# The second k-tile's weights split and multiplied by halves at the start of a hybrid encoder block

## The chip, the cores and the metric

The kernel runs on one core of one Trainium2 chip. The time is the device time of one execution in microseconds (us); less is better. A profiled execution gives the span, from the first to the last instruction that the profiler saw, and the times of single instructions.

## The reference

One encoder block over 512 tokens of width 2048: a modulated RMS norm, one input projection for two token mixers (dilated attention and gated linear attention), gates, an output projection and a final norm. The change touches only the first lines:

```python
mod = jax.nn.silu(c) @ w_cond[layer] + b_cond[layer]
shift, scale, gate = jnp.split(mod, 3, axis=-1)
h = rms_norm(x) * (1.0 + scale[:, None]) + shift[:, None]
proj = h @ w_in[layer]
```

The attention's values, 1024 of the columns of `proj`, are the first product that the kernel computes.

## The kernel before

Tokens lie transposed: 16 k-tiles of 128 features (on partitions) by 512 tokens. A float32 product is made of three matmuls on upper and lower parts (`hi`, `lo`, in the type that TensorE reads at once): upper tokens by upper weights, lower tokens by upper weights, upper tokens by lower weights. In the opening, "stage a", `h_hi` and `h_lo` hold the tokens times (1 + scale), without the norm and the shift, which come in later. For k-tile k this needs

- `sums(k, 0)` (on VectorE, DVE): the scale of the k-tile's 128 features, one reduction over a 128 x 2048 block of `w_cond` (`cb`, a load of 1 MB) against silu(c) (`sb`). For k = 0 it is done in four quarters.
- `u_high(k)` (on ScalarE, ACT) and `u_low(k)` (on DVE): the upper part `h_hi` and the rest `h_lo`. Both put the even tokens into the first 256 columns and the odd ones into the last.
- `w_high("a", k)` (ACT) and `w_low("a", k)` (DVE): the upper and lower part of the weights, 128 x 1024 from a load of 0.5 MB (`rawa`). For k = 0 these are two halves of 512 columns.
- `square(k)` (ACT) and `add_square(k)` (DVE): the sum of squares for the norm, used only at the end of the stage.

TensorE (PE) then does 24 matmuls of 128 x 512, into eight PSUM tiles that stay open over the 16 k-tiles: four groups of 128 tokens by two halves of 512 columns. For k-tile 0 `first_products(z, e)` does them by half z and by kind e (0: upper by upper, 1: lower tokens, 2: lower weights), four at a time; for the others `products("a", k, j)` does the three kinds of one PSUM tile, one after the other, in lines 228, 229 and 230.

Each engine runs its instructions strictly in the order in which the program lists them, and that order is made in advance by a planner, `_plan`. Every step is a task with an engine, an assumed duration, the tasks that it depends on, a priority, and a buffer pool from which it takes or to which it gives. `_plan` goes through time: whenever an engine is free, it takes the task of the highest priority among those that are ready at that moment; it never leaves an engine idle for a more urgent task that would be ready soon. A result is ready for another engine 0.2 us after its task ends, that of a load 0.9 us after. Loads (SP's queue) are planned in the same way, one at a time. The engines begin at PE 9.0, ACT 8.0, DVE 5.3, loads 5.0. The plan's times only make the order; on the chip semaphores hold the engines.

```python
for n in after[x]:
    left[n] -= 1
    e = tasks[n][0]
    lat = 0.0 if tasks[x][0] == e else 0.9 if tasks[x][0] == "DMA" else 0.2
    at[n] = max(at[n], now + lat)
...
for n in sorted(waiting[e], key=lambda n: -tasks[n][3]):
    _, dur, _, _, _, take, give = tasks[n]
    if at[n] > now + 1e-6 or (take and not free[take]):
        continue
```

Tasks are named `sum`, `uh`, `ul`, `wh`, `wl`, `sq`, `ss` (`add_square`) and `load`, `x`, `w` for the loads of `cb`, tokens and weights. By the code's own costs the loads of the opening are planned as `load` 1 (5.0), `x` 1 (8.1), `w` 1 (8.88), `load` 2 (10.43 to 13.53), `w` 2 (13.53), `x` 2 (15.08), `w` 3 (15.86 to 17.41), `load` 3 (17.41). DVE's plan: `sum` 0, `wl0` 0, `ul` 0, `wl0` 1, `sum` 1 (11.15), `wl` 1 (13.57), `ul` 1 (14.74), `sum` 2 (15.44), `wl` 2 (17.86), `ul` 2 (19.03), `ss` 1, `wl` 3 (20.38), `sum` 3 (21.55), `ss` 2, `ss` 3, `wl` 4 (25.27), `ul` 3 (26.44), `sum` 4 (27.14). ACT's: `wh0` 0 (8.0), `uh` 0, `wh0` 1, `sq` 0, `sq` 1, `wh` 1 (11.34), `uh` 1 (13.77), `wh` 2 (15.98), `sq` 2, `uh` 2 (18.06), `wh` 3 (18.72). A weight load has four buffers (`raw`), the split weights three (`whi`, `wlo`).

Of the kernel before, what the change touches and what calls it, by code (L numbers as in the profile page):

```python
# [10 lines left out]
F32 = mybir.dt.float32  # L11
F32R = mybir.dt.float32r
I32 = mybir.dt.int32
AF = mybir.ActivationFunctionType
# [4 lines left out]
P = 128  # L19
# [170 lines left out]
def block_kernel(ctx: ExitStack, tc: tile.TileContext, a: dict):  # L190
    nc = tc.nc
# [14 lines left out]
    def T2(name, dt=F32, parts=P):  # L206
        return t2.tile([parts, 512], dt, tag="t2", name=name)
# [10 lines left out]
    mm = nc.tensor.matmul  # L218
    tt = nc.vector.tensor_tensor
    stt = nc.vector.scalar_tensor_tensor  # L220
    act = nc.scalar.activation
# [60 lines left out]
    hot = T2("hot", F32R)  # L282
    onesr = cst.tile([P, P], F32R, tag="ones", name="ones")
# [15 lines left out]
    with tc.manual_schedule(engines=PLANNED):  # L299
        small_inputs()  # L300
        cond_load(0, 0)
        half_load(0)
        x_load(0)
        half_load(1)
        nc.scalar.preload_act_table_set("silu_and_others")
        nc.vector.memset(hot.bitcast(F32), 1.0)
        nc.vector.memset(epst, EPS)
        nc.vector.memset(ch.bitcast(F32), 0.0)
        nc.vector.memset(sel.bitcast(F32), 0.0)
        nc.gpsimd.memset(cl.bitcast(F32), 0.0)  # L310
        warm(5)

        nc.vector.tensor_copy(ch[:4], cin[:, :512])
        act(sel[:4], cin[:, 512:], AF.Copy)
        tt(cl[:4], cin[:, :512], ch[:4].bitcast(F32), op=ALU.subtract)

        nc.vector.tensor_scalar(bcond[:, 16:32], bcond[:, 16:32], 1.0, None, op0=ALU.add)
        nc.vector.tensor_copy(onesr, hot[:, :P].bitcast(F32))
        for j in range(4):
            spread(j, ch, True)  # L320
            spread(j, cl, False)
            act(sb[:, 512 * j:512 * j + 512], pcs[j], AF.Silu)
        warm(6)
# [31 lines left out]
    h_hi = hp.tile([P, KT, 512], F32R, tag="h", name="h_hi")  # L355
    h_lo = hp.tile([P, KT, 512], F32R, tag="h", name="h_lo")
# [7 lines left out]
    raws, wts, low, last = {}, {}, set(), {}  # L364
# [135 lines left out]
    def task(name, eng, dur, deps, prio, fn, take=None, give=None):  # L500
        tasks[name] = (eng, dur, deps, prio, fn, take, give)

    x_of = lambda k: xt[k // 4][:, k % 4, :]
    spl, psb, vraw, vv, sqs = {}, {}, {}, {}, {}
    scale = cst.tile([P, KT], F32, tag="scale", name="scale")
# [18 lines left out]
    def halves_of(t):  # L524
        return t.rearrange("p (a c) -> p a c", a=2)

    def parities_of(t):
        return t.rearrange("p (c a) -> p a c", a=2)

    def u_high(k):  # L530
        act(halves_of(h_hi[:, k, :]), parities_of(x_of(k)), AF.Copy, scale=scale[:, k:k + 1])

    def u_low(k):
        stt(halves_of(h_lo[:, k, :]), parities_of(x_of(k)), scale[:, k:k + 1], halves_of(h_hi[:, k, :].bitcast(F32)),
            op0=ALU.mult, op1=ALU.subtract)
# [3 lines left out]
        act(sqs[k], x_of(k), AF.Square)  # L539

    def add_square(k):
        tt(ssum, ssum, sqs.pop(k), op=ALU.add)

    def sum_row():
# [23 lines left out]
    def w_high(st, k, c=slice(0, 1024)):  # L568
        if (st, k) not in spl:
            spl[st, k] = [wp.tile([P, 1024], F32R, tag="w" + e, name=f"s{st}{k}{e}") for e in ("hi", "lo")]  # L570
        act(spl[st, k][0][:, c], start_w[st, k][:, c], AF.Copy)

    def w_low(st, k, c=slice(0, 1024)):
        hi, lo = spl[st, k]
        tt(lo[:, c], start_w[st, k][:, c], hi[:, c].bitcast(F32), op=ALU.subtract)

    def first_products(z, e):

        (wh, wl), hh, hl = spl["a", 0], h_hi[:, 0, :], h_lo[:, 0, :]
        c = slice(512 * z, 512 * z + 512)  # L580
        for i in range(4):
            j, t = 4 * z + i, slice(P * i, P * i + P)
            if e == 0:
                psb["a", j] = PJ(f"sta{j}") if j < 5 else PA(f"sta{j}")
            mm(psb["a", j], (hl if e == 1 else hh)[:, t], (wl if e == 2 else wh)[:, c], start=e == 0, stop=False)

    def products(st, k, j):
        if k == 0:
# [43 lines left out]
    for i, (st, k) in enumerate(sets[1:], 1):  # L632
        e = "ab".index(st)
# [6 lines left out]
    for k in range(KT):  # L640
        task(("sum", k, 0), "DVE", 2.42 if k else 3.4, [("load", k, 0)] + ([("ul", 0)] if k == 1 else []), 600 - 2 * k,
             lambda k=k: sums(k, 0), None, "b8")
        task(("uh", k), "ACT", 0.66, [("sum", k, 0), ("x", k)], 900 - k, lambda k=k: u_high(k))
        task(("ul", k), "DVE", 0.7, [("uh", k)], 900 - k, lambda k=k: u_low(k))
        task(("sq", k), "ACT", 0.56, [("x", k)] if k else [("uh", 0)], 700 - k, lambda k=k: square(k))
        if k:
            task(("ss", k), "DVE", 0.65, [("sq", 0), ("sq", k), ("ss", k - 1)], 300 - k,
                 lambda k=k: add_square(k))
    for z in range(2):
        c = slice(512 * z, 512 * z + 512)  # L650
        task(("wh0", z), "ACT", 0.66, [("uh", 0)] if z else [], 910, lambda c=c: w_high("a", 0, c),
             None if z else "wts")
        task(("wl0", z), "DVE", 0.69, [("wh0", z), ("sum", 0, 0)] + ([("ul", 0)] if z else []), 899,
             lambda c=c: w_low("a", 0, c), None, "raw" if z else None)

    behind = {("a", 1): [("wh0", 1), ("wl0", 1)], ("a", 2): [("wh0", 1), ("wl0", 1)], ("b", 1): [("hi", 0), ("lo", 0)],
              ("b", 2): [("wh", "b", 1), ("wl", "b", 1)], ("b", 3): [("wh", "b", 2), ("wl", "b", 2)]}
    for i, (st, k) in enumerate(sets):
        if not i:
            continue  # L660
        gh, gl = [[x] for x in behind[st, k]] if (st, k) in behind else ([], [])
        task(("wh", st, k), "ACT", 1.0, [("w", st, k)] + gh, 640 - i, lambda st=st, k=k: w_high(st, k), "wts")
        task(("wl", st, k), "DVE", 1.17, [("wh", st, k)] + gl, 640 - i, lambda st=st, k=k: w_low(st, k),
             None, "raw")
# [13 lines left out]
    for z in range(4):  # L678
        task(("row", z), "ACT", 0.9, [("uh", 7 + z), "rowl"], 50, lambda z=z: row_part(z // 2, z % 2))
    one_before = []  # L680
    for z in range(2):
        for e in range(3):
            name = ("mm", "a", 0, 7) if (z, e) == (1, 2) else ("m0", z, e)
            task(name, "PE", 1.2, one_before + [("uh", 0), ("wh0", z)] + [[], [("ul", 0)], [("wl0", z)]][e], 100, lambda z=z, e=e: first_products(z, e), None,
                 "wts" if (z, e) == (1, 2) else None)
            one_before = [name]
    for i in range(n):
        if i > 7:
            mm_task(i)
        st, k, j = chain[i]  # L690
        if k == KT - 1:
            task(("vo", j), "ACT", 0.54, [("mm", "a", k, j)], 950, lambda j=j: v_out(j))
# [13 lines left out]
    for i in range(n, 2 * n):  # L706
        mm_task(i)
        st, k, j = chain[i]
# [3 lines left out]
    for w in range(4):  # L712
        for kt in range(4):
            j, g = w // 2 * 4 + kt, w % 2
# [739 lines left out]
    for e in "hl":  # L1454
        t = hp.tile([P, KT, 512], F32R, tag="h", name="c_" + e)
# [318 lines left out]
```

## Time and profile before

| | |
|---|---|
| median of 3 runs | 910.82 us (909.99 to 911.43) |
| the profiled execution | 910.26 us, span 908.5 us |
| granted TensorE clock, mean | 0.997 |
| busy: PE, DVE, ACT, POOL | 894.6, 727.5, 492.9, 113.8 us |

In the lines shown below, PE is a matmul, PEld the load of its stationary operand, DVE VectorE, ACT ScalarE, POOL GpSimd, SP the queue that issues most loads. A line has the source line, the engine, the operation, and output <- inputs by the program's names with their shape. In the table of stretches the columns are the stretch, its length, busy time with the number of instructions of PE, PEld, DVE, ACT and POOL, the granted TensorE clock as a share of the full one, the busy share of the DMA engines, and GB/s. A busy PE is not PE at its peak, since the ends of matmuls are modelled; starts are what to compare.

### The profile page before, as it was taken

To read this page: it belongs to the slowest core of one execution; us is meant where nothing else is said; L and a number is where in the kernel's file an instruction comes from. 1 tells how busy PE (TensorE), PEld (TensorE's weight loads), DVE (VectorE), ACT (ScalarE), POOL (GpSimd) and SP (SyncE) were. 2 spreads that over 40 slices of the span, in tenths; PEclk is the share of its full clock that TensorE was granted. 3 is DMA by queue.
4 is the path that set the end of the run, shared out by engine and by line. 5 is a ranking of instruction groups with operands and counts; after the bars stand their busy time and mean duration, and the time that the engine had idled before them with its cause. 6 is when DMAs were issued, how large, how long until landed. Compare 5 with 4: busy or idle time off the path is not lost.

```text
span 908.5 us, 12576 instructions
## 1 busy us (share of the span) xinstructions
PE 894.6 (98%) x4295; PEld 746.9 (82%) x4295; DVE 727.5 (80%) x1235; ACT 492.9 (54%) x855; POOL 113.8 (13%) x203
## 2 busy tenths in 40 slices
PE   8999999999999999999999999999999999999996
PEld 6888888888888888888878888888888888888884
DVE  7988799878879888888659668495787559797797
ACT  5553533565655655655658554373654238455464
POOL 0000000023312222222100101111120100000001
PEclk9999999999999999999999999999999999999998
DMA  9999498588688898997878979778796987887863
GB/s 348 402 413 400 181 356 316 167 247 229 202 267 250 239 254 243 240 283 209 275 242 257 319 199 312 210 232 273 230 282 200 278 288 277 294 286 254 298 233 143
DMA packets 64203, 241.30 MB, mean 266 GB/s; under 512 B 8357, under 2 KB 10693, under 8 KB 54537
## 3 DMA queue, kind: packets, MB, share of 16 engines
q1 hardware_dynamic: 57378, 198.18, 61.1%
q0 software_dynamic: 6464, 42.01, 20.0%
q8 instruction: 34, 0.56, 0.2%
q10 hardware_dynamic: 296, 0.30, 0.1%
q14 instruction: 31, 0.25, 0.1%
HBM read 224.64 MB, written 51.47 MB: 304 GB/s over the span
## 4 chain that ended last, share of the span: by engine, by line
PE 92%; DVE 3%; ACT 2%; DMA 1%; issue 1%; SPq 0%; DVEq 0%; ACTq 0%
PE ps_qk L228 5%; PE ps_qk L229 5%; PE ps_qk L230 5%; PE g L230 4%; PE g L229 4%; PE g L228 4%; PE o L886 3%; PE stb L230 3%; PE stb L228 3%; PE stb L229 3%; PE ps_ag L228 3%; PE ps_ag L230 3%; PE ps_ag L229 3%; PE ps_gv_P L228 3%; PE ps_gv_P L229 3%; PE ps_gv_P L230 3%
## 5 line engine op out<-in xcount | busy, mean ns | idle before, releaser
L327 DVE CUSTOM_DVE_ANT_0 cb<-cb,sb,c_bcond 128x2048 f32<-128x2048 f32 (+1 forms) x32 | 73.4, 2295 | 0.3 <-DMA cb<-in_wm 0.3
L842 POOL TENSOR_SCALAR p<-p,st 128x416 f32<-128x416 f32 (+2 forms) x93 | 47.3, 516 | 175.2 <-DVE st L834 133.1
L831 ACT ACTIVATE p<-p,st 128x416 f32<-128x416 f32 x64 | 41.0, 641 | 39.5 <-DVE st L827 37.1
L861 ACT ACTIVATE pt<-t 128x384 fp32r<-128x384 f32 x64 | 31.2, 487 | 31.0 <-PE t L857 30.5
L428 POOL DMA_DIRECT2D T<-in_w_o x32 | 23.1, 723 | 157.9 <-ACT V2h L492 10.8
L886 PEld LDWEIGHTS o<-pt,vv 128*128 128x128 f32 x256 | 34.4, 189 | 4.2 <-DVE pt L862 1.7
L862 DVE TENSOR_TENSOR pt<-t,pt 128x384 fp32r<-128x384 f32 x64 | 35.1, 549 | 2.5 <-ACT pt L861 2.0
L886 PE MATMUL o<-pt,vv 128*128 128x256 f32 x256 | 35.9, 283 | 0.1
L857 PEld LDWEIGHTS t<-c_ident,p 128*128 128x128 f32 x192 | 24.8, 140 | 8.6
L857 PE MATMUL t<-c_ident,p 128*128 128x128 f32 x192 | 31.3, 272 | 0.0
L827 DVE CUSTOM_DVE_ANT_0 p<-s,g 128x160 f32<-128x160 f32 x64 | 23.5, 367 | 7.2 <-PE s L820 6.3
L827 DVE CUSTOM_DVE_ANT_0 p<-s,g,st 128x256 f32<-128x256 f32 x64 | 27.6, 431 | 1.6
L327 DVE CUSTOM_DVE_ANT_0 rawg<-rawg,crow,gate 128x1024 f32<-128x1024 f32 x16 | 20.4, 1280 | 4.1 <-DMA rawg<-in_wg 4.1
L820 PE MATMUL s<-ks,ql 128*128 128x416 f32 x64 | 22.5, 352 | 0.0
L819 PE MATMUL s<-ks,qh 128*128 128x416 f32 x64 | 22.5, 352 | 0.0
L1057 ACT ACTIVATE sq<-st,sc 128x256 f32<-128x256 f32 x24 | 12.2, 506 | 18.4 <-DVE st L1047 9.9
L428 POOL DMA_DIRECT2D T3V<-in_w_gv x8 | 5.5, 687 | 126.0 <-ACT qk21h L492 119.8
L1547 POOL TENSOR_SCALAR x<-x,rn 128x512 f32<-128x512 f32 x2 | 2.3, 1164 | 148.0 <-ACT rn L1536 143.6
L327 DVE CUSTOM_DVE_ANT_0 rawg<-rawg,crow,c_bcond 128x1024 f32<-128x1024 f32 x16 | 20.3, 1279 | 0.1
L877 DVE TENSOR_TENSOR pt<-r,pt 32x128 fp32r<-32x128 f32 x64 | 17.8, 279 | 1.9 <-ACT pt L875 1.3
L428 POOL DMA_DIRECT2D T<-T x16 | 9.1, 571 | 79.9 <-ACT V8h L492 12.9
L562 ACT ACTIVATE h_hi<-xt,shift 128x512 fp32r<-128x512 f32 x16 | 11.5, 719 | 12.9 <-DVE shift L327 12.9
(1660 smaller groups left out, 3129.6 us busy)
## 6 DMA issues: line engine op xcount, KB each, us to landing
cb<-in_wm SPq DMA_DIRECT2D x31, 1024.0 KB, 9.0
T<-in_w_o POOLq DMA_DIRECT2D x32, 512.0 KB, 6.6
rawg<-in_wg SPq DMA_DIRECT2D x32, 512.0 KB, 5.8
raw_O<-in_w_o SPq DMA_DIRECT2D x32, 512.0 KB, 4.4
raw_qk<-in_w_qk SPq DMA_DIRECT2D x24, 512.0 KB, 4.6
raw_O<-T SPq DMA_DIRECT2D x24, 512.0 KB, 5.0
rawb<-in_w_sb SPq DMA_DIRECT2D x16, 512.0 KB, 5.4
rawv<-in_wv SPq DMA_DIRECT2D x16, 512.0 KB, 4.4
```

The lines of the kernel that those rows point to most:

```text
L228: mm(ps, lh, rh, start=first, stop=False, skip_group_check=more)
L229: mm(ps, ll, rh, start=False, stop=False, skip_group_check=more)
L230: mm(ps, lh, rl, start=False, stop=last, skip_group_check=more)
L327: return nc.vector.tensor_tensor_reduce(out=w, in0=w, in1=with_, op0=ALU.mult, op1=ALU.add, scale=1.0, scalar=init, accum_out=dst)
L428: move = nc.gpsimd.dma_start(dst, src, max_dma_last_dim=8192, **how).ins
L827: top = nc.vector.tensor_tensor_reduce(out=t[:, lo:hi], in0=ps[:, lo:hi], in1=gt[h][:, at:at + 2 * (hi - lo) - 1:2], op0=ALU.add, op1=ALU.min,
L831: act(t, t, AF.Exp, bias=st[:, 0:1], scale=-1.0, accum_out=st[:, 1:2])
L842: last["pool"] = nc.gpsimd.tensor_scalar(to, of, st[:, 2:3], 1.0, op0=ALU.mult, op1=ALU.mult).ins
L857: nc.tensor.transpose(pk[:, kt * P:kt * P + P], t[:, first_ + kt * P:first_ + kt * P + P], ident)
L861: act(hi, src, AF.Copy)
L862: tt(lo, src, hi.bitcast(F32), op=ALU.subtract)
L886: mm(po[:, :256], vv[h // 4][:, CHUNK_OF[e][c], h % 4, :], t[:, w, c, :], start=n_ == 0 and w == 0, stop=n_ == 3 and w == 1)
```

## The change

The weights of k-tile 1 are split in two halves of 512 columns, as those of k-tile 0 were: tasks `wh1` and `wl1` take the place of `wh` and `wl` of k-tile 1. Its 24 matmuls are done by `first_products(1, z, e)`, half by half, four at a time, with the kinds in the order upper by upper, lower weights, lower tokens. `u_high` of k-tiles 0 and 1 becomes two instructions of 256 columns. The upper token part of k-tile 1 now also depends on the upper half 0 of its weights, the lower one on the lower half 0; the splits of k-tile 2 depend on those of half 1 of k-tile 1. The copy that makes the matrix of ones leaves the start of DVE's list and stands ahead of the first `add_square`; each `add_square(k)` now waits for `u_low(k)` in the plan.

```diff
--- before.py
+++ after.py
@@ -315,7 +315,6 @@
         tt(cl[:4], cin[:, :512], ch[:4].bitcast(F32), op=ALU.subtract)
 
         nc.vector.tensor_scalar(bcond[:, 16:32], bcond[:, 16:32], 1.0, None, op0=ALU.add)
-        nc.vector.tensor_copy(onesr, hot[:, :P].bitcast(F32))
         for j in range(4):
             spread(j, ch, True)
             spread(j, cl, False)
@@ -528,7 +527,9 @@
         return t.rearrange("p (c a) -> p a c", a=2)
 
     def u_high(k):
-        act(halves_of(h_hi[:, k, :]), parities_of(x_of(k)), AF.Copy, scale=scale[:, k:k + 1])
+        to, of = halves_of(h_hi[:, k, :]), parities_of(x_of(k))
+        for c in ((slice(0, 1), slice(1, 2)) if k < 2 else (slice(0, 2),)):
+            act(to[:, c], of[:, c], AF.Copy, scale=scale[:, k:k + 1])
 
     def u_low(k):
         stt(halves_of(h_lo[:, k, :]), parities_of(x_of(k)), scale[:, k:k + 1], halves_of(h_hi[:, k, :].bitcast(F32)),
@@ -539,6 +540,8 @@
         act(sqs[k], x_of(k), AF.Square)
 
     def add_square(k):
+        if k == 1:
+            nc.vector.tensor_copy(onesr, hot[:, :P].bitcast(F32))
         tt(ssum, ssum, sqs.pop(k), op=ALU.add)
 
     def sum_row():
@@ -574,15 +577,15 @@
         hi, lo = spl[st, k]
         tt(lo[:, c], start_w[st, k][:, c], hi[:, c].bitcast(F32), op=ALU.subtract)
 
-    def first_products(z, e):
-
-        (wh, wl), hh, hl = spl["a", 0], h_hi[:, 0, :], h_lo[:, 0, :]
+    def first_products(k, z, e):
+
+        (wh, wl), hh, hl = spl["a", k], h_hi[:, k, :], h_lo[:, k, :]
         c = slice(512 * z, 512 * z + 512)
         for i in range(4):
             j, t = 4 * z + i, slice(P * i, P * i + P)
-            if e == 0:
+            if e == k == 0:
                 psb["a", j] = PJ(f"sta{j}") if j < 5 else PA(f"sta{j}")
-            mm(psb["a", j], (hl if e == 1 else hh)[:, t], (wl if e == 2 else wh)[:, c], start=e == 0, stop=False)
+            mm(psb["a", j], (hl if e == 1 else hh)[:, t], (wl if e == 2 else wh)[:, c], start=e == k == 0, stop=False)
 
     def products(st, k, j):
         if k == 0:
@@ -640,11 +643,11 @@
     for k in range(KT):
         task(("sum", k, 0), "DVE", 2.42 if k else 3.4, [("load", k, 0)] + ([("ul", 0)] if k == 1 else []), 600 - 2 * k,
              lambda k=k: sums(k, 0), None, "b8")
-        task(("uh", k), "ACT", 0.66, [("sum", k, 0), ("x", k)], 900 - k, lambda k=k: u_high(k))
-        task(("ul", k), "DVE", 0.7, [("uh", k)], 900 - k, lambda k=k: u_low(k))
+        task(("uh", k), "ACT", 0.66, [("sum", k, 0), ("x", k)] + ([("wh1", 0)] if k == 1 else []), 900 - k, lambda k=k: u_high(k))
+        task(("ul", k), "DVE", 0.7, [("uh", k)] + ([("wl1", 0)] if k == 1 else []), 900 - k, lambda k=k: u_low(k))
         task(("sq", k), "ACT", 0.56, [("x", k)] if k else [("uh", 0)], 700 - k, lambda k=k: square(k))
         if k:
-            task(("ss", k), "DVE", 0.65, [("sq", 0), ("sq", k), ("ss", k - 1)], 300 - k,
+            task(("ss", k), "DVE", 0.65, [("sq", 0), ("sq", k), ("ss", k - 1), ("ul", max(k, 1))], 300 - k,
                  lambda k=k: add_square(k))
     for z in range(2):
         c = slice(512 * z, 512 * z + 512)
@@ -652,11 +655,15 @@
              None if z else "wts")
         task(("wl0", z), "DVE", 0.69, [("wh0", z), ("sum", 0, 0)] + ([("ul", 0)] if z else []), 899,
              lambda c=c: w_low("a", 0, c), None, "raw" if z else None)
-
-    behind = {("a", 1): [("wh0", 1), ("wl0", 1)], ("a", 2): [("wh0", 1), ("wl0", 1)], ("b", 1): [("hi", 0), ("lo", 0)],
+        task(("wh1", z), "ACT", 0.66, [("w", "a", 1), ("uh", 1) if z else ("wh0", 1)], 901, lambda c=c: w_high("a", 1, c),
+             None if z else "wts")
+        task(("wl1", z), "DVE", 0.69, [("wh1", z), ("ul", 1) if z else ("wl0", 1)], 898.5,
+             lambda c=c: w_low("a", 1, c), None, "raw" if z else None)
+
+    behind = {("a", 2): [("wh1", 1), ("wl1", 1)], ("b", 1): [("hi", 0), ("lo", 0)],
               ("b", 2): [("wh", "b", 1), ("wl", "b", 1)], ("b", 3): [("wh", "b", 2), ("wl", "b", 2)]}
     for i, (st, k) in enumerate(sets):
-        if not i:
+        if (st, k) in (("a", 0), ("a", 1)):
             continue
         gh, gl = [[x] for x in behind[st, k]] if (st, k) in behind else ([], [])
         task(("wh", st, k), "ACT", 1.0, [("w", st, k)] + gh, 640 - i, lambda st=st, k=k: w_high(st, k), "wts")
@@ -678,14 +685,15 @@
     for z in range(4):
         task(("row", z), "ACT", 0.9, [("uh", 7 + z), "rowl"], 50, lambda z=z: row_part(z // 2, z % 2))
     one_before = []
-    for z in range(2):
-        for e in range(3):
-            name = ("mm", "a", 0, 7) if (z, e) == (1, 2) else ("m0", z, e)
-            task(name, "PE", 1.2, one_before + [("uh", 0), ("wh0", z)] + [[], [("ul", 0)], [("wl0", z)]][e], 100, lambda z=z, e=e: first_products(z, e), None,
-                 "wts" if (z, e) == (1, 2) else None)
-            one_before = [name]
+    for k in range(2):
+        for z in range(2):
+            for e in ((0, 1, 2), (0, 2, 1))[k]:
+                name = ("mm", "a", k, 7) if (z, e) == (1, 2 - k) else ("m", k, z, e)
+                task(name, "PE", 1.2 if k == 0 else 0.91, one_before + [("uh", k), (f"wh{k}", z)] + [[], [("ul", k)], [(f"wl{k}", z)]][e],
+                     100, lambda k=k, z=z, e=e: first_products(k, z, e), None, "wts" if (z, e) == (1, 2 - k) else None)
+                one_before = [name]
     for i in range(n):
-        if i > 7:
+        if i > 15:
             mm_task(i)
         st, k, j = chain[i]
         if k == KT - 1:
```

## The prediction

> **What bounds the kernel now.** I read the page first, then the waits of PE, then the opening in stretches, then each engine's timeline there. In the timelines the columns are start, duration, engine, line, instruction, and in brackets the idle time just before with its releaser.
>
> ```profile
> span 908.5 us, 12576 instructions
> ...
> PE 894.6 (98%) x4295; PEld 746.9 (82%) x4295; DVE 727.5 (80%) x1235; ACT 492.9 (54%) x855; POOL 113.8 (13%) x203
> ...
> PE 92%; DVE 3%; ACT 2%; DMA 1%; issue 1%; SPq 0%; DVEq 0%; ACTq 0%
> ```
> ```profile
> PE sta L585 <- ACT h_hi L531: 2.1, 1, 2.1
> PE warm L294 <- DVE hot L306: 1.5, 1, 1.5
> PE sta L229 <- DVE h_lo L534: 0.7, 1, 0.7
> PE go L1089 <- ACT V27h L492: 0.3, 1, 0.3
> ```
> ```profile
> 10.17:15.75 5.58, 5.58 (x24) 4.61 (x25) 4.56 (x5) 3.34 (x5) 0.00 (x0) 1.00 1.01 413
> 15.75:28.10 12.35, 11.56 (x50) 8.94 (x48) 12.24 (x15) 6.20 (x8) 0.00 (x0) 1.00 1.03 415
> 28.10:60.00 31.90, 31.90 (x141) 26.41 (x142) 30.23 (x33) 17.72 (x30) 0.69 (x1) 1.00 1.02 405
> ```
>
> TensorE carries 92% of the chain that ended last, and of its named waits only 0.3 us lies behind the opening. From 28.10 to 60 us it is busy for 31.90 of 31.90 us. So what the change is worth is the move of one moment: when PE enters its last unbroken run, at about 28 us. In 15.75 to 28.10 VectorE (the third engine of the row) is busy for 12.24 of 12.35 us and the DMA share is full: there DVE's order decides.
>
> ```profile
> 10.17 1.20 PE L585 MATMUL sta<-sa0hi,h_hi 128*128 128x512 f32 x4 [2.13 <-ACT h_hi L531]
> 11.20 1.08 PE L585 MATMUL sta<-sa0hi,h_lo 128*128 128x512 f32 x4
> ...
> 15.75 0.40 PE L228 MATMUL sta<-sa1hi,h_hi 128*128 128x512 f32 x1
> 16.82 0.50 PE L229 MATMUL sta<-sa1hi,h_lo 128*128 128x512 f32 x1 [0.67 <-DVE h_lo L534]
> ```
> ```profile
> 27.59 0.39 PE L228 MATMUL sta<-sa3hi,h_hi 128*128 128x512 f32 x1
> 28.10 0.49 PE L229 MATMUL sta<-sa3hi,h_lo 128*128 128x512 f32 x1
> 28.44 0.39 PE L230 MATMUL sta<-sa3lo,h_hi 128*128 128x512 f32 x1
> ```
>
> From 11.20 to 15.75 twenty matmuls start: 0.2275 us each, 5.46 us for the 24 of a k-tile. The second matmul of k-tile 1 should start at 15.98 and starts at 16.82, 0.84 late, for the low token part `h_lo`. In k-tile 3 the second starts 0.28 late, again for `h_lo`, and the next follows after 0.34 instead of 0.23. PE without that wait would have begun k-tile 3 at 28.44 - 2 x 0.2275 = 27.98; this is the moment I compare.
>
> **The order after the change.** Each engine's order comes from the planner in the code, from costs and due times written there, so I worked the changed tasks through by hand (plan times, which only give the order). Sum 1 ends on DVE at 13.57 as before. ACT splits half 0 of the second weights from 11.34 to 12.00; DVE takes their low half from 13.57 to 14.26. The upper token part runs on ACT from 13.77 to 14.43, so the low token part `ul` 1 is ready at 14.63. But the third modulation load ends at 13.53 and with its 0.9 makes sum 2 ready at 14.43. DVE is idle from 14.26, and the planner never holds an engine back for a more urgent task: it takes sum 2 (2.42) at 14.43, and `ul` 1, though of priority 899 against 596, comes behind it. Before, the undivided low part kept DVE until 14.74, when `ul` 1 was ready, and `ul` 1 went first. So DVE's new order is: low half 0, sum 2, `ul` 1, low half 1, `ul` 2, the moved copy and sum of squares, low part of k-tile 3, that of k-tile 2, sum 3, a sum of squares, low part 4, `ul` 3. Tile 3 comes ahead of 2 because the split of tile 2 now waits for low half 1 (ready at 18.44) and that of tile 3 for its load (18.31), ACT being idle.
>
> **Part by part, on the chip's rows.**
>
> ```profile
> 5.66 0.22 DVE L318 CAST ones<-hot 128x128 fp32r<-128x128 f32 x1
> 5.89 0.75 DVE L327 CUSTOM_DVE_ANT_0 cb<-cb,sb,c_bcond 128x512 f32<-128x512 f32 x1
> ...
> 9.24 0.69 DVE L575 TENSOR_TENSOR sa0lo<-rawa,sa0hi 128x512 fp32r<-128x512 f32 x1
> ```
> ```profile
> 9.36 0.76 ACT L531 ACTIVATE h_hi<-xt,scale 128x512 fp32r<-128x512 f32 x1 [1.22 <-DVE scale L327]
> ...
> 13.78 1.06 ACT L571 ACTIVATE sa1hi<-rawa 128x1024 fp32r<-128x1024 f32 x1 [0.64 <-DMA rawa<-in_w_sa]
> 14.75 0.75 ACT L531 ACTIVATE h_hi<-xt,scale 128x512 fp32r<-128x512 f32 x1
> ...
> 19.74 1.05 ACT L571 ACTIVATE sa3hi<-rawa 128x1024 fp32r<-128x1024 f32 x1
> ```
> ```profile
> L616 ACT ACTIVATE vv<-vraw,rcol 128x256 fp32r<-128x256 f32 x16 | 7.0, 495 | 0.0
> ```
>
> *Copy moved.* The first sum starts up to 0.22 earlier, and with it the chain to 9.36 (bounds 0 and 0.22; I take 0.18). *Token halves.* The nearest row for a half is the 128x256 at 0.495; two of them end some 0.14 to 0.24 later than one of 0.76, but the first matmuls read only half 0: PE starts at 9.18 + 0.50 + 0.05 = 9.73 instead of 10.17. The second half ends at 9.18 + 0.40 + 0.50 = 10.08 (ACT's steps overlap by 0.1, as 14.75 against 13.78 + 1.06 shows), `h_lo` some 0.8 later, and its product starts at 10.9 instead of 11.20. So k-tile 1 can begin at 10.9 + 4.55, about 15.5 instead of 15.75. *Weight halves.* The second weights still land at 13.76; half 0 is split by 14.40 and its low half by 15.1; the token halves end at 15.2. So the first eight matmuls of k-tile 1 (upper tokens with high and low weights) run from 15.5 to 17.3. The new order puts the `h_lo` product after them, 8 x 0.2275 = 1.8 us more room than before.
>
> ```profile
> SPq L273 <- DMA cb<-in_wm: 2.2, 1, 2.2
> ```
> ```profile
> 11.83 2.35 DVE L327 CUSTOM_DVE_ANT_0 cb<-cb,sb,c_bcond 128x2048 f32<-128x2048 f32 x1 [0.33 <-DMA cb<-in_wm]
> ...
> 14.88 1.22 DVE L575 TENSOR_TENSOR sa1lo<-rawa,sa1hi 128x1024 fp32r<-128x1024 f32 x1 [0.69 <-ACT sa1hi L571]
> 16.02 0.74 DVE L534 SCALAR_TENSOR_TENSOR h_lo<-xt,scale,h_hi 128x512 fp32r<-128x512 f32 x1
> 16.68 2.34 DVE L327 CUSTOM_DVE_ANT_0 cb<-cb,sb,c_bcond 128x2048 f32<-128x2048 f32 x1
> ...
> 18.95 1.22 DVE L575 TENSOR_TENSOR sa2lo<-rawa,sa2hi 128x1024 fp32r<-128x1024 f32 x1
> ...
> 20.76 0.68 DVE L542 TENSOR_TENSOR ssum<-ssum,sq 128x512 f32<-128x512 f32 x1
> 21.36 1.22 DVE L575 TENSOR_TENSOR sa3lo<-rawa,sa3hi 128x1024 fp32r<-128x1024 f32 x1
> ```
>
> *The wait that is added.* Sum 2 needs its 1 MB load. In the stretch 15.5 to 16.7 SP's queue has one wait, for such a load; its next issue starts at 16.29, so that load landed about 16.28 (bounds for sum 2's start: 16.3, and 16.68 where it stood). DVE, in order, stands idle from 15.1 with the finished `h_hi` of tile 1 behind it. Sum 2 holds DVE for 2.27 (16.68 to 18.95): to 18.58. `ul` 1 then ends at 19.33, and PE starts its product at 19.40: a new wait of 19.40 - 17.3 = 2.1 us. What was won earlier, the copy and the token halves, ends in this wait and is worth nothing.
>
> *Behind it.* PE: 13 matmuls are left of 16, counted from 19.40 with 0.34 for the first step: k-tile 2 at 19.40 + 0.34 + 15 x 0.2275 = 23.15 (before, 22.15). DVE from 18.58, by start-to-start steps of the rows: `ul` 0.66, low half about 0.65, `ul` 0.66, copy 0.22, squares 0.60, low part of tile 3 1.14, then that of tile 2, 1.22 long: it ends at 23.7, where PE wants it two matmuls into the tile, at 23.6. So 0.16 more and a restart of 0.11: k-tile 3 at 23.15 + 5.46 + 0.27 = 28.88. `h_lo` of tile 3 is due at 29.1; DVE ends it at 23.65 + 2.27 + 0.60 + 1.14 + 0.75 = 28.4: that old wait is gone. Sum: 28.88 - 27.98 = **+0.9 us**. Bounds: sum 2 at 16.68 adds 0.4; low part 2 on time takes 0.2 off, and 0.3 later adds that; together +0.4 to +1.6.
>
> ```profile
> 17.62 0.33 SPq L267 DMA_DIRECT2D rawa<-in_w_sa  x1
> ```
> ```profile
> 29.45 1.06 ACT L571 ACTIVATE sa5hi<-rawa 128x1024 fp32r<-128x1024 f32 x1 [1.69 <-DMA rawa<-in_w_sa]
> ```
>
> *What is hidden.* The load of tile 5's weights, issued at 17.62, reuses the buffer of tile 1's, which is now released at about 20.0. SP waits there, and a modulation load and a token load behind it. Weights issued at 17.62 land near 29.4, so some 11 us of transfers stand ahead, and a stall of 2.4 us lets none run dry: zero; were that cover gone, 2.4. In the later k-tiles the sums of squares trail by one tile on DVE; the same number of steps stand in a tile, so zero. The last one still ends before the row sum, which waits for an eviction.
>
> [...] PE was idle for 2.13 us ahead of 10.17, and its next four matmuls took 1.03 instead of 0.91 us: that restart, 0.12, is what I charge. [...]
>
> The profiled execution took 910.26 us (span 908.5 and 1.76 around it), so 911.2; the median of the three runs is 910.82, 0.56 higher, so the runs should have a median of **911.7**.
>
> **The rivals.**
> 1. *`ul` 1 runs ahead of sum 2*, as its priority suggests, and the change does what its words say. Then nothing waits in k-tiles 1 and 2. On DVE the copy (0.22) and the second half (2 x 0.69 against 1.22) are about paid for by half 0 being ready 0.44 before 14.88, so the steps behind keep their times but for one sum of squares fewer (0.7) ahead of this one:
>
> ```profile
> 27.30 0.75 DVE L534 SCALAR_TENSOR_TENSOR h_lo<-xt,scale,h_hi 128x512 fp32r<-128x512 f32 x1
> ```
> It then ends at 27.35 instead of 28.05, and PE loses 0.7 less at k-tile 3: 910.1. Against it: the 0.2 us by which the planner finds sum 2 ready first.
> 2. *The buffers of split weights go round in allocation order* (slower). Three buffers serve them; tile 3 is now split ahead of 2. If tile 5 gets the buffer of tile 3 and not of the one first free, ACT stands at its split until PE ends k-tile 3 at 34.3; the split ends at 35.4, its low part on DVE at 36.6 and `h_lo` of tile 4 behind that at 37.3, 2.8 after it is due (34.6). With a restart +3.8: 914.6. It decides only if that buffer comes free later than 29.4, when the weights land.
>
> ```profile
> 44.37 1.06 ACT L571 ACTIVATE sa8hi<-rawa 128x1024 fp32r<-128x1024 f32 x1 [1.57 <-PE sta L229]
> ```
> Such a wait exists, off the path here; that releases are taken in order of time speaks against the rival, as the planner counts them so.
> 3. *The clock falls in the new wait.* The opening shows both rates:
>
> ```profile
> 5.18 0.57 PE L297 MATMUL pc<-c_lo,sel 128*128 128x512 f32 x1
> 5.58 0.39 PE L297 MATMUL pc<-c_hi,sel 128*128 128x512 f32 x1
> 5.81 0.39 PE L297 MATMUL pc<-c_lo,sel 128*128 128x512 f32 x1
> ```
> 0.40 a matmul until 5.58, 0.23 from there, 4.1 us after PE began (its first wait ended at 1.5). A second such spell loses 4.1 x (1 - 0.23/0.40) = 1.7: +2.6, 913.4. The 2.13 us that left no such spell speak against it.
>
> **How the numbers follow.** A measurement of this kernel can tell about 0.2%, 1.8 us, from no change. Forecast 0.72, rival 1 0.11, rival 2 0.08, rival 3 0.04, something not named 0.05. The forecast lies inside 1.8 us but for 0.02 above it; rival 1 but for 0.01 below; rivals 2 and 3 are slower; the unnamed goes 0.02, 0.02, 0.01. Faster 0.03, same 0.82, slower 0.15. The range takes in the forecast's own bounds (911.2 to 912.4), rival 1 and the runs' spread, 0.8 us either way: 909.9 to 913.2; rivals 2 and 3 stay out.
>
> **What would show it.** Right: on DVE the 128x2048 sum of k-tile 2 starts near 16.3 ahead of `h_lo` of tile 1; PE waits about 2 us for that `h_lo` after the first eight matmuls of k-tile 1; no PE wait at k-tile 3, which begins near 28.8; PE starts near 9.7. Wrong: `h_lo` of tile 1 before 16.3, a k-tile 3 that begins before 28.0, a wait of ACT on PE near 29 to 34, or matmuls 0.4 apart behind the wait.

## The result and the profile after

The changed kernel took 912.51 us (median of 21 runs, 911.15 to 915.23), the kernel before 911.05 in the same series (21 runs, 909.99 to 912.20). The ratio is 1.0017, 95% interval 1.0010 to 1.0025: slower by about 1.5 us. The interval is clear of 1, but the difference is still below the 0.2% (1.8 us) under which the prediction spoke of no change. The forecast was 911.7, its range 909.9 to 913.2. The profiled execution took 912.51 us. From its page:

```profile
span 910.5 us, 12568 instructions
...
PE 896.2 (98%) x4295; PEld 745.9 (82%) x4295; DVE 727.8 (80%) x1236; ACT 493.9 (54%) x858; POOL 113.9 (13%) x203
...
PE 91%; DVE 3%; DMA 3%; ACT 1%; issue 1%; SPq 0%; DVEq 0%; ACTq 0%
```

All of PE's named waits after the change (us in total, times, longest):

```profile
PE sta L588 <- ACT h_hi L532: 1.7, 1, 1.7
PE sta L588 <- DVE h_lo L535: 1.5, 1, 1.5
PE warm L294 <- DVE hot L306: 1.5, 1, 1.5
PE go L1097 <- ACT V27h L491: 0.3, 1, 0.3
```

The 0.7 us for `h_lo` in k-tile 3 is gone; 1.5 for another `h_lo` stands in its place. DVE's timeline in the opening shows which, and why:

```profile
14.39 0.69 DVE L578 TENSOR_TENSOR sa1lo<-rawa,sa1hi 128x512 fp32r<-128x512 f32 x1 [0.25 <-ACT sa1hi L574]
16.22 2.35 DVE L326 CUSTOM_DVE_ANT_0 cb<-cb,sb,c_bcond 128x2048 f32<-128x2048 f32 x1 [1.14 <-DMA cb<-in_wm]
18.50 0.08 DVE L326 DVE_READ_ACCUMULATOR2_ANT scale<- 128x1 f32 x1
18.50 0.74 DVE L535 SCALAR_TENSOR_TENSOR h_lo<-xt,scale,h_hi 128x512 fp32r<-128x512 f32 x1
...
20.50 0.75 DVE L535 SCALAR_TENSOR_TENSOR h_lo<-xt,scale,h_hi 128x512 fp32r<-128x512 f32 x1
21.17 1.22 DVE L578 TENSOR_TENSOR sa2lo<-rawa,sa2hi 128x1024 fp32r<-128x1024 f32 x1
22.30 1.22 DVE L578 TENSOR_TENSOR sa3lo<-rawa,sa3hi 128x1024 fp32r<-128x1024 f32 x1
```

DVE stands idle for 1.14 us for the load of sum 2, although ACT has finished `h_hi` of tile 1 at about 15.2; the sum then holds it for 2.28, and `h_lo` of tile 1 starts at 18.50. On PE (timeline):

```profile
16.69 1.07 PE L588 MATMUL sta<-sa1lo,h_hi 128*128 128x512 f32 x4
19.30 1.20 PE L588 MATMUL sta<-sa1hi,h_lo 128*128 128x512 f32 x4 [1.54 <-DVE h_lo L535]
...
23.07 0.39 PE L228 MATMUL sta<-sa2hi,h_hi 128*128 128x512 f32 x1
...
28.50 0.39 PE L228 MATMUL sta<-sa3hi,h_hi 128*128 128x512 f32 x1
28.73 0.39 PE L229 MATMUL sta<-sa3hi,h_lo 128*128 128x512 f32 x1
28.96 0.39 PE L230 MATMUL sta<-sa3lo,h_hi 128*128 128x512 f32 x1
```

PE waits after eight matmuls of k-tile 1; k-tile 3 begins at 28.50 without a wait, 0.52 after the 27.98 that the prediction counted for before. This is what the two traces show of the opening: +0.5, where +1.5 was measured.

**A measure for the opening.** The first loads do not land at one time in all executions. So I read the openings against one event: the moment ACT starts to split the second weights, which is when they have landed (13.73 here, 13.78 before, 14.88 in e8). The first matmul of k-tile 6 comes 30.56 us after it before (44.34 - 13.78), and 31.10 after the change (44.83 - 13.73). Below, "k-tile 6 after the split" is this number. The rows are ACT's after the change (the one before stands in the prediction) and PE's, before and then after:

```profile
13.73 0.63 ACT L574 ACTIVATE sa1hi<-rawa 128x512 fp32r<-128x512 f32 x1 [0.64 <-DMA rawa<-in_w_sa]
14.27 0.94 ACT L532 ACTIVATE h_hi<-xt,scale 128x256 fp32r<-128x256 f32 x2
```
```profile
44.34 0.39 PE L228 MATMUL sta<-sa6hi,h_hi 128*128 128x512 f32 x1
```
```profile
44.83 0.39 PE L228 MATMUL sta<-sa6hi,h_hi 128*128 128x512 f32 x1
```

### The profile page after: what moved, and what is told of

Its sections match the earlier page's. It is cut to its first block, busy times and chain, and to the rows that moved or that the text cites. A ratio compares the mean times of both kernels' runs of the same rounds, so it can differ in the third digit from the quotient of the medians.

```text
span 910.5 us, 12568 instructions
## 1 busy us (share of the span) xinstructions
PE 896.2 (98%) x4295; PEld 745.9 (82%) x4295; DVE 727.8 (80%) x1236; ACT 493.9 (54%) x858; POOL 113.9 (13%) x203
## 4 chain that ended last, share of the span: by engine, by line
PE 91%; DVE 3%; DMA 3%; ACT 1%; issue 1%; SPq 0%; DVEq 0%; ACTq 0%
PE ps_qk L229 5%; PE ps_qk L228 5%; PE ps_qk L230 5%; PE g L230 4%; PE g L229 4%; PE g L228 4%; PE o L894 3%; PE stb L230 3%; PE stb L229 3%; PE stb L228 3%; PE ps_ag L230 3%; PE ps_ag L228 3%; PE ps_ag L229 3%; PE ps_gv_P L228 3%; PE ps_gv_P L229 3%; PE ps_gv_P L230 3%
## 5 line engine op out<-in xcount | busy, mean ns | idle before, releaser
L464 DVE TENSOR_TENSOR raw_O<-raw_O,raw_P 128x1024 f32<-128x1024 f32 x8 | 9.8, 1225 | 12.6 <-DMA raw_O<-in_w_o 8.8
```

## The experiments

Theory at the outset: sum 2 ahead of `ul` 1 on DVE makes the wait, worth 0.5 us in the opening, and something else adds about 0.9 in the median. In the page's chain DMA rose from 1% to 3%, so the first candidate was the late loads of `raw_O`; the rival was the clock. In the table, the ratio to the kernel before is that of the series, not the quotient of the two medians.

| kernel | median us (runs) | before beside it (runs) | ratio, 95% interval | k-tile 6 after the split |
|---|---|---|---|---|
| changed, again | 912.80 (11) | 911.51 (33) | 1.0011 (1.0001 to 1.0021) | 31.12 |
| e1, `ul` 1 first | 911.55 (11) | 911.51 | 1.0000 (0.9991 to 1.0009) | 30.60 |
| e2, copy and sums later only | 911.38 (11) | 911.51 | 0.9998 (0.9988 to 1.0008) | 30.15 |
| e4, two matmuls more | 911.85 (11) | 911.51 | 1.0006 (0.9997 to 1.0014) | 31.00 |
| e5, the wait filled | 912.34 (11) | 911.39 (20) | 1.0013 (1.0003 to 1.0022) | 31.12 |
| e6, k-tile 1 by kinds | 910.79 (11) | 911.39 | 0.9995 (0.9986 to 1.0004) | 30.18 |
| e7a, changed, one load fewer | 911.94 (11) | 911.41 (35) | 1.0010 (1.0001 to 1.0018) | 32.62 |
| e7b, before, one load fewer | 910.94 (11) | 911.41 | 0.9998 (0.9990 to 1.0007) | 30.54 |
| e8, e6 with more warm-up | 910.88 (11) | 911.41 | 0.9993 (0.9984 to 1.0001) | 29.44 |
| e9, before with more warm-up | 911.32 (12) | 911.41 | 0.9997 (0.9988 to 1.0005) | 30.55 |

**The changed kernel again.**

> The changed kernel once more, for a second profile and for times beside the other kernels. Theory (order): the planner's new order, sum 2 ahead of ul 1 on DVE, costs about 0.5 us of PE in the opening in every execution (k-tile 3 begins at 28.5 instead of 27.98), and what the median has beyond that, some 0.9 us, lies in waits of the output projection for its loads (raw_O, raw_P), which differ from execution to execution: the opening is the same to 0.1 us, the offset of PE's matmuls stays flat from 30 to 780 us, and only the steps behind 780 us differ from those of the first profile (+0.6 at 789 and +0.7 at 865). Rival (lengthened sums of squares): the moved sums of squares and the copy make later k-tiles or the change to stage b late too: then the offset grows between 30 and 120 us. Rival (noise): the opening itself varies by 0.5 us.

It gave 912.80, and 31.12 in the opening: the difference stands, and so does the gap between 0.55 in the opening and 1.3 in the median. Theory's other signs are there too: from 30 to 780 us PE's distance to the kernel before is flat to 0.1 us, and what differs from the first profile lies in two steps behind that, at about 789 and 870 us (0.67 us together here, 1.49 in the first profile).

**e1: the wait taken away by order.** On the changed kernel, sum 2 also waits for `ul` 1 in the plan (the list of what a sum waits for, cut out of its line):

```
-  [("load", k, 0)] + ([("ul", 0)] if k == 1 else [])
+  [("load", k, 0)] + ([("ul", k - 1)] if k in (1, 2) else [])
```

> The changed kernel with one dependency more: sum 2 waits for ul 1 in the plan, as sum 1 did for ul 0; nothing else. Theory (order): PE's wait of 1.5 us in k-tile 1 is gone, k-tile 3 begins at 27.2 to 27.6 (before 27.98, after 28.50), and the time falls by 0.9 to 1.3 us against the changed kernel and to 0.4 to 0.8 below the kernel before, if the late loads add nothing. Rival (the instructions themselves): the second halves and the split tokens cost the 0.5 us; then k-tile 3 begins no earlier than 28.0 and the time stays at or above that of the kernel before.

The wait in k-tile 1 and the 0.5 are gone (30.60, before 30.56): the cause of the opening's loss is shown. The median is back at that of the kernel before as well, and e1's interval (0.9991 to 1.0009) lies below that of the first series of the changed kernel (1.0010 to 1.0025), though it overlaps that of the second (1.0001 to 1.0021). The gain that rival 1 hoped for, and the expected 0.4 to 0.8 us below the kernel before, is not there. PE's waits of e1, and its DVE:

```profile
PE sta L229 <- DVE h_lo L535: 0.8, 1, 0.8
```
```profile
16.34 2.35 DVE L326 CUSTOM_DVE_ANT_0 cb<-cb,sb,c_bcond 128x2048 f32<-128x2048 f32 x1
18.61 0.08 DVE L326 DVE_READ_ACCUMULATOR2_ANT scale<- 128x1 f32 x1
18.61 1.22 DVE L578 TENSOR_TENSOR sa2lo<-rawa,sa2hi 128x1024 fp32r<-128x1024 f32 x1
20.47 1.23 DVE L578 TENSOR_TENSOR sa3lo<-rawa,sa3hi 128x1024 fp32r<-128x1024 f32 x1 [0.64 <-ACT sa3hi L574]
21.61 0.75 DVE L535 SCALAR_TENSOR_TENSOR h_lo<-xt,scale,h_hi 128x512 fp32r<-128x512 f32 x1
```

Two low parts now run ahead of `h_lo` of tile 2, which starts at 21.61; PE wants it about 21.4. The wait has moved by one k-tile.

**e2: the other half of the change alone.** Before, with the copy in the second `add_square` step and each sum of squares behind `ul` in the plan:

```
+        if k == 1:
+            nc.vector.tensor_copy(onesr, hot[:, :P].bitcast(F32))
-  [("sq", 0), ("sq", k), ("ss", k - 1)]
+  [("sq", 0), ("sq", k), ("ss", k - 1), ("ul", max(k, 1))]
```

> The kernel before with the last part of the change alone: the copy to the matrix of ones stands ahead of the first sum of squares, and each sum of squares waits for ul of its k-tile in the plan. Theory (order): the order of sum 2 and ul 1 stays as before, one sum of squares fewer stands ahead of ul 3, so the late start in k-tile 3 (0.28 and 0.11 of restart) is gone and the time falls by 0.3 to 0.4; the rest is unchanged. Rival (lengthened sums of squares): the trailing sums and the copy cost the 0.5 us of the opening or widen the late waits: then the time rises by 0.5 or more.

30.15 against 30.56: this half wins 0.41 in the opening, the old wait of k-tile 3. The median does not tell it from nothing. So, if the two parts simply add, the halves of the second k-tile cost about 0.95 us in the opening, and this part gives 0.4 of it back.

**e4: is lateness itself dear?** Before, with two matmuls of k-tile 3 issued twice:

```
+            if k == 3 and j < 2:
+                mm(ps, hh[:, t], wh[:, c], start=False, stop=False)
```

> The kernel before, but two matmuls of k-tile 3 (upper by upper, of the first two PSUM tiles) are done twice, so that PE is 0.46 us later from there on; the attention's values are wrong by that. Theory (order): a later PE passes through to the end one for one: +0.46. Rival (late loads): what the median has beyond the opening comes from PE's lateness itself, because the loads of the output projection then fall worse: +1.2 to +1.6.

+0.44 in the opening, +0.34 in the median. A delay at k-tile 3 passes through about one for one; that a late kernel meets worse late waits is not supported, though the median's interval (-0.3 to 1.3 us) reaches the lower end of that rival.

**e5, e6 and two more profiles of the changed kernel.** e5 fills PE's new wait with seven more matmuls in k-tile 1; e6 is e2 with the weights of k-tile 1 undivided, its eight outputs multiplied by kinds (upper by upper, then the low weights, then the low tokens) and the low part of tile 4's weights planned behind `ul` 3.

```
+        for i in range(7 if (k, z, e) == (1, 0, 2) else 0):
+            mm(psb["a", i % 4], hh[:, ...], wh[:, c], start=False, stop=False)
```

> The changed kernel, and PE does seven more matmuls (upper by upper of k-tile 1 again) between its eighth product of k-tile 1 and the product of the lower tokens, 1.6 us of the 2.2 us in which it otherwise stands; the attention's values are wrong by that. No other engine has more to do. Theory (clock): of the 32 times of the changed kernel so far 14 lie above 913, 6 of them with a mean granted clock of 0.995; in these executions the clock falls to half for some us at PE's wait. Filled, the wait leaves no such execution: no time above 913.3, median 911.6 to 912.1, structure unchanged (k-tile 3 starts 14.8 us after the second weights' split starts). Rival (late loads): the high times come from the loads of the output projection and the first loads; then the median stays at 912.5 to 912.8 and three to six of eleven times lie above 913.

> A version meant to beat both: the kernel before, with the copy and the sums of squares later (as in the run that moved those alone), the 24 matmuls of k-tile 1 by kind (eight upper by upper, eight with the low weights, eight with the lower tokens), its weights undivided, and the low part of tile 4's weights planned behind ul 3. Theory (order): the lower tokens of tile 1 are wanted 3.6 us later, so PE does not wait in k-tile 1, and ul 3 comes 1.1 us earlier on DVE, so it does not wait in k-tile 3: k-tile 3 begins 13.0 to 13.4 us after the split of the second weights starts (before 14.2, changed 14.8), time 0.8 to 1.1 us below the kernel before. Rival (loads): PE then stands in k-tile 2 or 4 for a load, and the gain is under 0.4.

> The changed kernel, one more profile. Theory (clock): if this execution takes over 913 us, its records show a stretch of half clock behind PE's wait in k-tile 1, with matmuls about 0.43 apart. Rival (late loads): PE's steps behind 780 us are then larger than in the first two profiles, and matmuls behind the wait stay 0.2275 apart.

> As the run before it: the changed kernel, one more profile. Theory (clock): over 913 us goes with matmuls 0.43 apart behind PE's wait in k-tile 1. Rival (late loads): over 913 us goes with larger steps behind 780 us.

e5 left PE a wait of 0.4 us and gave +0.95. Its median of 912.34 lies above what the clock theory said (911.6 to 912.1), and three of its eleven times lie above 913.2 (913.48, 913.53, 913.71), against 13 of 32 in the two series of the changed kernel. The theory had said none above 913.3, so this forecast of it failed; of the rival's signs, the median of 912.5 to 912.8 was not met, the three to six times over 913 were. Eleven runs are too few to tell the shares apart, so e5 settles nothing by itself. e6 came to 910.79, 0.6 below the kernel before instead of 0.8 to 1.1, and its k-tile 3 began 13.86 after the split instead of 13.0 to 13.4. In two of these profiles PE ran at half clock for one spell, ahead of k-tile 1. Such a stretch of half clock is called a spell below. The stretches of e6, and of the first of the two profiles (PE busy and its matmuls first, granted clock behind the engines):

```profile
8.00:11.73 3.73, 1.41 (x6) 1.17 (x7) 3.09 (x7) 2.42 (x4) 0.00 (x0) 1.00 1.01 408
11.73:15.15 3.42, 3.42 (x10) 2.65 (x9) 2.36 (x2) 1.24 (x2) 0.00 (x0) 0.50 1.02 426
```
```profile
8.00:11.60 3.60, 1.72 (x6) 1.13 (x7) 3.06 (x7) 2.62 (x5) 0.00 (x0) 1.00 1.00 402
11.60:15.01 3.41, 3.41 (x9) 2.65 (x9) 2.99 (x4) 1.89 (x4) 0.00 (x0) 0.50 1.02 426
```

In both spells eight matmuls start, 0.43 us apart, where fifteen would at 0.2275; the table also counts those that reach into the stretch. In that first profile of the two (912.99 us) the loss ended in the wait of k-tile 1 (31.10 after the split all the same). The other (911.99 us) had no spell (31.09). Neither took over 913 us, so the case that the two expectations speak of was not caught.

**e7a and e7b: the late loads against the clock.** Both kernels without the second load of the output weights that are a sum of two blocks:

```
-            second[gi["O", s]] = block_load(out_tile(s + 1, f"raw_P{s}"), pair, "12", g)
```

> The changed kernel without the second load and its sum for the weights of product P5 in the output projection (raw_P; eight loads of 512 KB and eight sums fewer): P5 uses one block where it should use the sum of two. With its twin below this takes away the place at which PE's offset grew behind 780 us. Theory (late loads): what the changed kernel has beyond its opening comes from there; the median of this kernel is 0.4 to 0.8 above that of its twin, and its times lie within 2 us. Rival (elsewhere): the distance to the twin stays at 1.2 to 1.5 and times over 2.5 us above its fastest remain.

> The kernel before without the second load and its sum for the weights of product P5, as in the twin above (P5 uses one block where it should use the sum of two). Theory (late loads): PE's last matmul comes 870.5 to 871.3 us after k-tile 3 begins, in both twins alike; the time falls by 0.5 to 2 against the kernel before. Rival (elsewhere): the twins differ there by 0.5 or more.

The twins differ by 1.00 us. If the late loads made the rest of the difference, the twins should differ by the opening's 0.55 alone; with intervals of some 0.8 us either way on each twin, the medians do not decide that. e7a's times spread over 3.2 us and two lie more than 2.5 above its fastest, as the rival said; e7b's median fell by 0.5, which its interval does not tell from nothing. The late parts of their profiles agree, as expected: from the start of k-tile 3 (counted without its wait) to PE's last matmul 871.28 us in e7a and 871.33 in e7b. What e7a's profile shows besides is the prediction's third rival. PE's timeline, and the stretches around it:

```profile
16.99 1.07 PE L587 MATMUL sta<-sa1lo,h_hi 128*128 128x512 f32 x4
20.23 2.07 PE L587 MATMUL sta<-sa1hi,h_lo 128*128 128x512 f32 x4 [2.18 <-DVE h_lo L534]
22.11 1.71 PE L587 MATMUL sta<-sa1hi,h_hi 128*128 128x512 f32 x4
23.66 1.08 PE L587 MATMUL sta<-sa1lo,h_hi 128*128 128x512 f32 x4
```
```profile
16.64:20.05 3.41, 1.42 (x7) 0.84 (x5) 2.90 (x3) 1.63 (x4) 0.00 (x0) 1.00 1.05 426
20.05:23.46 3.41, 3.23 (x8) 2.55 (x9) 3.41 (x7) 1.56 (x2) 0.00 (x0) 0.50 1.02 410
23.46:30.00 6.54, 6.54 (x30) 5.40 (x29) 6.54 (x7) 3.09 (x4) 0.00 (x0) 1.00 1.02 409
```

Four matmuls take 1.9 us from start to start instead of 0.91, and k-tile 6 stands 32.62 after the split instead of 31.10. By the equal late parts nothing gives these 1.5 us back. This execution took 913.25.

**e8 and e9: more warm-up.** The second warm-up of PE goes from 6 to 14 matmuls, so that PE is not idle ahead of k-tile 0; e8 on e6, e9 on before.

```
-        warm(6)
+        warm(14)
```

> The version by kinds with eight more of the matmuls on ones that PE does while it waits for the first scale (14 instead of 6), so that it stands for 0.3 to 0.6 us instead of 2.1 before the first product. In the profile of the version by kinds the clock was at half for one spell of 3.4 us in k-tile 0, and k-tile 1 began at 17.53 instead of about 16.3. Theory (clock): no such spell comes, k-tile 1 begins when its weights are split, k-tile 3 begins 13.0 to 13.3 us after the split of the second weights starts, and the median is 0.3 to 0.8 below that of the version by kinds and 0.8 to 1.3 below the kernel before. Rival (loads): nothing changes, since DVE sets k-tile 3: 13.8 us and the same median.

> The kernel before with 14 instead of 6 of the matmuls on ones ahead of the first product, nothing else. Theory (clock): a spell of half clock in k-tile 0 costs the kernel before about 0.9 us where it falls (k-tile 1's second matmul is late anyway by 0.84), in perhaps a third of the executions; the median falls by 0 to 0.3 and the mean granted clock of 0.995 disappears. Rival: the matmuls on ones run into the first product and the time rises by 0.1 to 0.4.

Neither profile shows a spell. e9's opening is that of before (30.55), and 0.1 us in the median is not told from nothing. e8's named waits of PE in the opening are two, and k-tile 3 begins 12.78 after the split (27.66 - 14.88; before 14.20, counted):

```profile
PE warm L294 <- DVE hot L306: 1.5, 1, 1.5
PE sta L592 <- ACT h_hi L530: 0.7, 1, 0.7
```

Part of that 1.4 is lost again in k-tile 4, whose `h_lo` is now late by some 0.2 (29.44 against 30.56 at k-tile 6: 1.1 kept). The median is 0.5 us below before, where 0.8 to 1.3 was expected, with an interval that just reaches 1; against the changed kernel, by the ratios to before, it is faster (0.9984 to 1.0001, against 1.0010 to 1.0025 in the first series of the changed kernel). It is the best version with e6; that it beats the kernel before is likely, not shown.

## Why the prediction was right, and where it was not

**Right, and seen.** Sum 2 runs ahead of `ul` 1 (16.22, forecast 16.3). `h_lo` of tile 1 starts at 18.50 (18.58). PE resumes at 19.30 after its first eight matmuls of k-tile 1 (19.40) and starts k-tile 2 at 23.07 (23.15). The old wait of k-tile 3 is gone. Tile 5's load stands on SP for its buffer, as worked out, in SP's waits:

```profile
SPq L267 <- DVE sa1lo L578: 2.4, 1, 2.4
```

and its cover held. Behind k-tile 3 PE is as unbroken as before:

```profile
28.50:60.00 31.50, 31.50 (x140) 26.09 (x139) 29.51 (x34) 17.82 (x30) 0.68 (x1) 1.00 1.02 405
60.00:95.00 35.00, 35.00 (x156) 28.98 (x155) 30.15 (x32) 14.38 (x22) 0.51 (x1) 1.00 0.97 382
```

**Wrong: what was won ahead of the wait.** The prediction let k-tile 1 begin at 15.5, 0.25 earlier than before, and lost that in the new wait. In fact PE began at 9.91 (forecast 9.73, before 10.17), but the product of tile 0's `h_lo` came at 11.12 (11.20 before) and took a longer first step again, so k-tile 1 began at 15.79, against 15.75 before. Nothing won reached the wait, and the wait was 1.54 us, not 2.1. The end of the wait is set by DVE, so the sum does not change by this.

**Wrong in size: the copy.** I took 0.18 for moving it; the first sum starts at 5.86 instead of 5.89, so 0.03. The copy was not what the sum waited for. Two halves of `h_hi` on ACT took 0.95 together, against 0.76 for the whole. Neither term reaches the end.

**Wrong step: tile 3 ahead of tile 2 on DVE.** I had the split of tile 2 wait for low half 1. In the code only its low part does; the split waits for the upper half. So `sa2lo` came at 21.17, ahead of `sa3lo`, in time, and the 0.27 that I charged in k-tile 2 did not arise. With 0.1 more from `h_lo` and the steps behind it, this makes +0.52 in the opening instead of +0.9.

**Wrong chance: the clock.** Rival 3 names what e7a's profile shows, at nearly the right price (1.7 forecast, 1.5 measured), but it got 0.04 because a wait of 2.13 us before had left no spell. The step that failed took one wait without a spell to speak for all of about its length: 2.13 us before left the granted clock at 1.00, and 2.18 in e7a were followed by 3.41 us at 0.50. PE was busy for 1.42 us in the 3.41 us ahead of e7a's spell (16.64 to 20.05). Before, the wait lay across these two stretches, with 2.50 and 2.20:

```profile
5.54:8.96 3.42, 2.50 (x11) 1.69 (x9) 2.98 (x9) 2.25 (x5) 0.00 (x0) 1.00 1.03 353
8.96:12.37 3.41, 2.20 (x10) 1.82 (x11) 2.86 (x6) 1.80 (x3) 0.00 (x0) 1.00 1.00 407
```

In the changed kernel's profiled execution, with its wait of 1.54 us, PE was busy for 1.88, and the clock stayed at 1.00:

```profile
16.18:19.60 3.42, 1.88 (x8) 1.26 (x8) 3.38 (x4) 2.10 (x3) 0.00 (x0) 1.00 1.07 427
19.60:23.01 3.41, 3.41 (x16) 2.80 (x15) 3.41 (x6) 1.47 (x3) 0.00 (x0) 1.00 1.01 405
```

But the busy time does not order all cases: 1.72 us in 3.60 (8.00 to 11.60) stood ahead of the spell in the first of the two later profiles of the changed kernel, and in e7b 1.66 in 3.42 (7.14 to 10.56) left the clock at 1.00 until 13.97. What decides was not shown; the two lengths above lie 0.05 us apart.

**Rivals 1 and 2.** e1 is rival 1 made: +0.04 at k-tile 6, not -0.7. Its k-tile 2 begins 7.57 us after the split instead of 8.37, and the wait for tile 2's `h_lo` takes that back. Rival 2's wait of ACT on PE near 29 to 34 did not occur.

**The sum, and what is open.** The measured time lies in the range, but not by the sum. In the opening the change cost 0.55 where 0.9 was charged (e1 takes it away); the remaining 0.5 to 0.9 of the median comes from behind it or from spells, which the sum had at nothing. That these two errors partly cancel is luck.

How often a spell fell can be estimated from the runs, since each lists its mean granted clock. In the profiles before and after, PE's last matmul starts 9.2 us ahead of the end of the span (at 899.26 and 901.28), and the clock is at 0.50 from 4.0 and 2.4 us behind it to the end. Those 5.23 and 6.87 us alone make the means of 0.997 and 0.996. The eleven profiles without a spell list 0.996 to 0.998; a spell of 3.41 us at half takes another 0.0019, and the three with one list 0.995 or 0.996. So, by this estimate, a run at 0.997 or more had no spell, one at 0.995 had one, and 0.996 can be either. The 34 runs of the changed kernel, and the 88 of the kernel before that list a clock:

| granted clock | changed: runs, median us, over 913 us | before: runs, median us, over 913 us |
|---|---|---|
| 0.997 and more | 11, 911.53, 1 | 64, 911.36, 2 |
| 0.996 | 16, 912.86, 8 | 20, 911.50, 0 |
| 0.995 | 7, 914.30, 5 | 4, 913.46, 3 |

In the runs at 0.997 and more the changed kernel is 0.2 us above the kernel before (-0.2 to 0.7 by resampling), which leaves room for the opening's 0.55 and for little more. What its median has beyond that lies in the runs of a lower clock, 23 of 34 against 24 of 88 before. e1, which takes the new wait away, has none at 0.995 in eleven runs; nor have e8 and e9, with more warm-up, in 23. (Before has four in 88, fewer than the third that the expectation of e9 took; and of the long runs that the expectation of e5 counts at 0.995 there are five, not six.)

So the remainder goes with spells, but that they are its whole cause is not shown. Only e7a's profile shows a spell behind the new wait, and with a load left out; the one spell that was profiled in the changed kernel itself lay ahead of that wait. One spell can take half of 3.41 us, 1.7, and the runs at 0.995 lie 2.8 above those at 0.997 and more. And of e5's three long times, with the wait filled, two list 0.995 and one 0.997, so by the same estimate a long time needs no spell.

The late loads are the other part. Behind the opening, all differences between the profiled executions arise in two steps of PE, at about 789 and 870 us; from 36 to 780 us its distance to the kernel before is flat to 0.15 us in every trace. Against the profile before, the steps add up to 0.7 to 2.0 us in the four profiles of the changed kernel, 0.9 in e1 and 1.0 in e5, and to 0.3 to 0.8 in e2, e4, e6 and e8 and 1.4 in e9, which do not halve the second k-tile. In e7a and e7b, without the second load, they are gone (0.05 or less; the profile before happens to have none either). So, as far as two profiles can show it, these loads make the steps, in every kernel; whether the change makes them worse, some 0.6 us on average here, too few profiles tell. Waits of DVE for them, before and then after:

```profile
DVE raw_O L465 <- DMA raw_P<-in_w_o: 4.7, 4, 1.6
DVE raw_O L465 <- issue: 2.9, 1, 2.9
DVE raw_O L465 <- DMA raw_O<-in_w_o: 2.8, 3, 1.3
```
```profile
DVE raw_O L464 <- DMA raw_O<-in_w_o: 8.8, 4, 3.9
DVE raw_O L464 <- DMA raw_P<-in_w_o: 3.7, 4, 1.6
```

From k-tile 3 to PE's last matmul it took 871.28 us before and 872.78 after in the first profiles, and 871.92 to 873.22 in the three others of the changed kernel. Executions of one kernel differ there by about as much as the medians do, and the twins, with the load gone, keep 1.00 of the difference.

## What to carry to other kernels

A planner that never holds an engine back can turn "ready a little earlier" into a loss: halving a task freed DVE 0.5 us sooner, a 2.3 us job that stood second moved ahead, and the urgent one came last. Work out the new order on each engine, not only the new durations, and check each dependency by the name in the code. And read the granted clock behind a gap on PE, not only the gap's length: a gap of 2.13 us before left it at 1.00, one of 2.18 us in e7a was followed by 3.41 us at 0.50, and k-tile 6 came 1.5 us later.

## What the hardware showed that was not expected

In 3 of 14 profiles the granted clock stood at 0.50 for a spell of 3.41 or 3.42 us in the opening: from 11.73 us in e6, from 11.60 in the first of the two later profiles of the changed kernel, from 20.05 in e7a. The longest wait of PE ahead of each was 2.58, 2.15 and 2.18 us; 2.13 us before left the clock at 1.00. Why a spell followed those three waits and not this one, these profiles do not show.

The second weights' split started at 13.73 us after the change, at 13.78 before and at 14.88 in e8; the openings here are compared after that is taken out.
